# A priority offset of 200 for what side streams emit, in a two-block fp32 transformer kernel on one core

## The chip, the cores and the metric

One core of a Trainium2 chip. The metric is the device time of one execution in microseconds (us). TensorE is PE in the rows (its weight loads PEld), VectorE is DVE, ScalarE is ACT, GpSimd is POOL, SyncE is SP; every DMA of the kernel is issued from SP's queue.

## What is computed

A sequence of 256 tokens of width 1024, all in float32, goes through two blocks. Cut to what matters:

```
first_block:  cols = rmsnorm(x) @ w_in
              ya = rwkv7_time_mix(cols)       # 8 heads of 64, state S_t = S_{t-1} diag(w_t) + (S_{t-1} a_t) b_t^T + v_t k_t^T
              yb = diff_attention(cols)       # 4 heads, softmax(a) - lam * softmax(b), ALiBi
              x += (gates * (ya @ w_proj_a, yb @ w_proj_b)) @ w_out
              x += relu(rmsnorm(x) @ w_ff1)**2 @ w_ff2      # 1024 -> 4096 -> 1024
              x  = rmsnorm(x + gated per-layer embedding)
second_block: for layer in 0, 1:
                x += 0.5 * swiglu(rms_norm(x))              # 1024 -> 2816 -> 1024
                x += attention(rms_norm(x))   # layer 0: stick-breaking, MoBA; layer 1: forgetting, dilated; q and k normed and rotated
                x += 0.5 * swiglu(rms_norm(x))
```

## The kernel before

The 256 tokens are two tiles of 128. Each product with a weight matrix is three matmuls (`mm3`, which calls `mm`, L279): weight and activation are each split into a high and a low part, and hi by hi, hi by lo and lo by hi are summed in PSUM. Weights come in units of 128 x 1024 floats (512 KB). `wunit` (L336) issues the DMA into one of three `raw` buffers (L341), and `split` makes `hi` on ACT (L365) and `lo` on DVE (L366). There are five pairs of hi and lo buffers during the first mix, eleven after it. In the trace the same two lines also split the transposed activations (hTh, hTl).

The main stream is these products. What lies between them, the elementwise work of the two mixes and of the attentions with its small matmuls and transposes (`tr`, L283), is written as generators, the side streams. `Weave` (L126 to L205) keeps them: `spawn` (L163) starts one, `pump` takes the stream that is due first and lets `step` (L143) run it to its next `yield`, and `mm` calls for that as planned time passes. So the program order is a braid of main and side streams, which the planner's own clock makes.

PE runs in exactly the program's order, since a manual schedule is set for it. DVE, ACT, POOL and SP don't: the framework's scheduler orders their instructions, and among those that it deems ready it takes the one of highest priority, which is the one that stands first in the program. Once built, each engine's order is fixed, and an engine waits for the next instruction in its order, whatever else is ready behind it. Some streams are started before anything else, and some of what they emit is loads: `Mix.setup` (L1061, constants `fv`, `w2a`, `k_mix`, `g`), `setup_late` (L1096, `row_sub`), `bf_const` (`cb_alibi`, L308). The first activations are loaded in `first_part` (L1550, L1552), normed into `h` (L909) and transposed.

Names used below: `kk`, `c`, `AR`, `BK` and `X` belong to the time mix (`prepare`, L1174, and the inverse, L1267 on), `UV` to its chain over chunks (L1355), `oa` to its output (L1384, L1404), `gate` to the gates ahead of w_out (L1542, L1659), `qk` and `Q` to the first mix too (L1413, L1284). In the second block `qk_norm` (L542) norms q and k of one token tile (L548 to L565; its rotation `rb` is on POOL, L562 and L563), and `softmax_side` (L649) makes the weights that PE then transposes (maxima `m` L678, masked weights L685). Token tile 0 of that step in layer 1 has the tile w__11067, tile 1 has w__11112, and the first softmax tiles are w__11203 and w__11204; in layer 0 tile 1 is w__6776. `forget_sums` (L567) makes `fx` and `lf`.

Of the kernel before, what the change touches and what calls it, by code (L numbers as in the profile page):

```python
# [108 lines left out]
class Mark:  # L109


    def __init__(self):
        self.done, self.at, self.res = False, 0.0, None
# [8 lines left out]
class Weave:  # L122
# [20 lines left out]
    def step(self, s):  # L143
        t = self.t
        try:
            v = next(s.gen)
        except StopIteration as e:
            self.credit -= self.t - t
            self.finish(s, e.value or 0.0)
            if s in self.sides:  # L150
                self.sides.remove(s)
            return
        self.credit -= self.t - t
        s.wait, s.due = (), self.t
        if isinstance(v, float):
            s.due += v
        else:
            s.wait = tuple(v)
# [60 lines left out]
class Ker:  # L219


    def __init__(self, ctx, tc, d):
        self.tc, self.nc, self.d = tc, tc.nc, d
        nc = self.nc
        ctx.enter_context(tc.manual_schedule(engines={mybir.EngineType.PE}))
        self.W = Weave()
        self.const = ctx.enter_context(tc.tile_pool(name="const", bufs=1))
        self.xp = ctx.enter_context(tc.tile_pool(name="xp", bufs=1))
        self.act = ctx.enter_context(tc.tile_pool(name="act", bufs=2))
        self.ps = ctx.enter_context(tc.tile_pool(name="ps", bufs=1, space=PSUM))  # L230
        self.banks = Slots(self.W, self.ps, "b", [128, 512], 8)
        self.quota, self.held = 2, 0
        self.x = [self.xp.tile([128, D], F32, name=f"x{t}") for t in range(2)]
        self.pre = None
# [548 lines left out]
    def attn_layer(self, pool, hT, layer, after):  # L783
# [64 lines left out]
        for step, g in ATTN_ORDER:  # L848
            if step == "qk":
                queries(g, GROUPS.index(g))  # L850
            else:
                vms.setdefault(g, Mark())
                values(g)
# [100 lines left out]
def attn_plan(layer):  # L954
    win = "w_in_ab_2" if layer == 0 else "w_in_cd_2"
    out = []
    for step, g in ATTN_ORDER:
        a, b = g * 256, g * 256 + 256
        if step == "qk":
            out.append(((win, 0, ("qk", g)), (0, D), [(a, b), (D + a, D + b)]))  # L960
        else:
            more = [(3 * D, 3 * D + 8)] if layer == 1 and g == GROUPS[0] else []
            out.append(((win, 0, ("v", g)), (0, D), [(2 * D + a, 2 * D + b)] + more))
    for g in GROUPS:
        out.append((("w_out_2", layer, g), (g * 256, g * 256 + 256), [(0, D)]))
    return out
# [53 lines left out]
def mix_plan():  # L1020
    def attend(i):
        a, b = 1792 + i * 128, 1792 + i * 128 + 128
        return (("w_in", 0, ("at", i)), (0, D), [(a, b), (512 + a, 512 + b), (1024 + a, 1024 + b)])

    out = [attend(0), (("w_in", 0, "wg"), (0, D), [(1536, 1792)])]
    for j in range(4):
        a, b = j * 128, j * 128 + 128
        out.append((("w_in", 0, ("kr", j)), (0, D), [(512 + a, 512 + b), (a, b)]))
    for j in range(2):
        out.append((("w_in", 0, ("v", j)), (0, D), [(1024 + j * 256, 1280 + j * 256)]))  # L1030
    for step, i in MIX_ORDER:
        out.append(attend(i) if step == "at" else (("w_in", 0, ("gt", i)), (0, D), [(3328 + i * 512, 3840 + i * 512)]))
    out.append((("w_proj_b", 0, 0), (0, 512), [(0, D)]))
    out.append((("w_proj_a", 0, 0), (0, 512), [(0, D)]))
    out.append((("w_out", 0, 0), (0, D), [(0, D)]))
    return out
# [817 lines left out]
```

## Time and profile before

| | us |
|---|---|
| median of 3 runs | 1529.46 (1527.96 to 1530.95) |
| the profiled execution | 1529.78 |
| its span | 1528.0 |
| PE busy | 1489.4 (97%) |
| DVE busy | 927.9 (61%) |
| ACT busy | 760.8 (50%) |
| POOL busy | 46.7 (3%) |
| mean granted clock of PE | 0.994 |

The span runs from the first to the last instruction of the profile; the profiled execution's own time has 1.78 us around it. A row of the timeline gives start, duration, engine, line, operation, output and inputs with their sizes, and, in brackets, the idle time of the engine just before and what ended it.

### The profile page before, as it was taken

To read this page: it belongs to the slowest core of one execution; us is meant where nothing else is said; L and a number is where in the kernel's file an instruction comes from. 1 tells how busy PE (TensorE), PEld (TensorE's weight loads), DVE (VectorE), ACT (ScalarE), POOL (GpSimd) and SP (SyncE) were. 2 spreads that over 40 slices of the span, in tenths; PEclk is the share of its full clock that TensorE was granted. 3 is DMA by queue.
4 is the path that set the end of the run, shared out by engine and by line. 5 is a ranking of instruction groups with operands and counts; after the bars stand their busy time and mean duration, and the time that the engine had idled before them with its cause. 6 is when DMAs were issued, how large, how long until landed. Compare 5 with 4: busy or idle time off the path is not lost.

```text
span 1528.0 us, 22440 instructions
## 1 busy us (share of the span) xinstructions
PE 1489.4 (97%) x8804; PEld 1237.2 (81%) x8804; DVE 927.9 (61%) x1528; ACT 760.8 (50%) x1142; POOL 46.7 (3%) x70
## 2 busy tenths in 40 slices
PE   7999989999999999999999999999999999999999
PEld 6887767788888788887888888887888888888887
DVE  5886777755558755557546554566545787565552
ACT  6644445644536544447565444445444566464441
POOL 1120100000000000001100000000000010000000
PEclk9999999999999999999999999999999999999999
DMA  7233238655544765536434665547555444275551
GB/s 253 90 118 107 98 119 278 202 194 177 182 151 157 223 200 190 185 132 193 138 111 147 198 194 192 179 156 220 190 189 182 141 154 136 78 227 180 179 182 53
DMA packets 76298, 254.97 MB, mean 167 GB/s; under 512 B 11040, under 2 KB 13344, under 8 KB 76192
## 3 DMA queue, kind: packets, MB, share of 16 engines
q1 hardware_dynamic: 76192, 253.53, 51.1%
q8 instruction: 69, 1.13, 0.3%
q14 instruction: 37, 0.30, 0.1%
HBM read 252.45 MB, written 1.05 MB: 166 GB/s over the span
## 4 chain that ended last, share of the span: by engine, by line
PE 81%; DVE 7%; DMA 5%; ACT 4%; issue 2%; POOL 0%; SPq 0%; ACTq 0%; DVEq 0%; POOLq 0%
PE b L279 77%; DMA raw<-in_w_dram 4%; PE b L283 4%; DVE lo L366 2%; ACT hi L365 2%; DMA grow<-in_norm_mix_g_dram 0%; DMA stage<-in_consts_dram 0%; DMA lam<-in_lam_k_dram 0%; POOL rb L563 0%; POOL rb L562 0%; DVE hTl L366 0%; DVE c L1132 0%; DVE U L1260 0%; DVE u L1129 0%; ACT e L376 0%
## 5 line engine op out<-in xcount | busy, mean ns | idle before, releaser
L366 DVE TENSOR_TENSOR lo<-raw,hi 128x1024 fp32r<-128x1024 f32 (+1 forms) x465 | 561.9, 1214 | 356.1 <-ACT hi L365 350.1
L365 ACT ACTIVATE hi<-raw 128x1024 fp32r<-128x1024 f32 (+1 forms) x465 | 485.6, 1050 | 417.4 <-PE b L279 207.6
L279 PE MATMUL b<-hi,hTh 128*128 128x512 f32 (+2 forms) x1312 | 499.9, 381 | 0.7 <-ACT hi L365 0.7
L279 PE MATMUL b<-hi,hTl 128*128 128x512 f32 (+2 forms) x1312 | 489.9, 373 | 0.5 <-DVE hTl L366 0.5
L279 PE MATMUL b<-lo,hTh 128*128 128x512 f32 (+2 forms) x1312 | 489.7, 373 | 0.8 <-DVE lo L366 0.8
L279 PEld LDWEIGHTS b<-hi,hTl 128*128 128x128 f32 x1312 | 247.4, 189 | 47.8 <-DVE hTl L366 0.9
L279 PEld LDWEIGHTS b<-hi,hTh 128*128 128x128 f32 x1312 | 247.6, 189 | 46.1 <-issue 2.5
L279 PEld LDWEIGHTS b<-lo,hTh 128*128 128x128 f32 x1312 | 247.8, 189 | 44.2 <-DVE lo L366 1.5
L279 PE MATMUL b<-hi,aTh 128*128 128x512 f32 x480 | 191.6, 399 | 0.0
L279 PE MATMUL b<-hi,aTl 128*128 128x512 f32 x480 | 188.1, 392 | 0.0
L279 PE MATMUL b<-lo,aTh 128*128 128x512 f32 x480 | 187.4, 390 | 0.0
L279 PEld LDWEIGHTS b<-hi,aTl 128*128 128x128 f32 x480 | 90.1, 188 | 20.1
L279 PEld LDWEIGHTS b<-lo,aTh 128*128 128x128 f32 x480 | 90.3, 188 | 18.0
L279 PEld LDWEIGHTS b<-hi,aTh 128*128 128x128 f32 x480 | 90.2, 188 | 17.6
L463 ACT ACTIVATE a<-b,rsi_x 128x512 f32<-128x512 f32 (+1 forms) x52 | 34.4, 662 | 55.3 <-PE b L279 55.2
L365 ACT ACTIVATE aTh<-b 128x512 fp32r<-128x512 f32 (+1 forms) x64 | 36.3, 567 | 43.2 <-PE b L283 41.8
L465 DVE SCALAR_TENSOR_TENSOR a<-b,rsi_x,a 128x512 f32<-128x512 f32 (+1 forms) x52 | 37.2, 716 | 32.1 <-PE b L279 17.3
L366 DVE TENSOR_TENSOR aTl<-b,aTh 128x512 fp32r<-128x512 f32 (+1 forms) x64 | 41.8, 653 | 20.0 <-ACT aTh L365 19.7
L279 PE MATMUL b<-hi,hT1h 128*128 128x512 f32 (+1 forms) x128 | 53.4, 418 | 0.0
L279 PE MATMUL b<-lo,hT1h 128*128 128x512 f32 (+1 forms) x128 | 47.8, 373 | 0.6 <-DVE lo L366 0.6
L279 PE MATMUL b<-hi,hT1l 128*128 128x512 f32 (+1 forms) x128 | 47.4, 371 | 0.0
L365 ACT ACTIVATE hTh<-b 128x512 fp32r<-128x512 f32 (+1 forms) x48 | 25.2, 541 | 38.1 <-PE b L283 33.5
(582 smaller groups left out, 1293.6 us busy)
## 6 DMA issues: line engine op xcount, KB each, us to landing
raw<-in_w_dram SPq DMA_DIRECT2D x446, 512.0 KB, 4.2
raw<-in_w_dram SPq DMA_DIRECT2D x16, 384.0 KB, 3.4
grow<-in_norm_ffn_dram SPq DMA_DIRECT2D x4, 512.0 KB, 5.3
x<-in_x_dram SPq DMA_DIRECT2D x4, 256.0 KB, 6.2
x<-in_x_dram SPq DMA_DIRECT2D x2, 512.0 KB, 4.4
grow<-in_norm_mix_dram SPq DMA_DIRECT2D x2, 512.0 KB, 4.8
out_dram<-x SPq DMA_DIRECT2D x4, 256.0 KB, 2.0
raw<-in_w_dram SPq DMA_DIRECT2D x2, 396.0 KB, 3.6
```

The source lines that it names most:

```text
L279: self.nc.tensor.matmul(out=out, lhsT=lhsT, rhs=rhs, start=start, stop=stop, skip_group_check=skip)
L283: self.nc.tensor.transpose(out=out, in_=src, identity=self.ident)
L365: self.nc.scalar.activation(out=hi, in_=src, func=AF.Copy)
L366: self.nc.vector.tensor_tensor(out=lo, in0=src, in1=hi.bitcast(F32), op=ALU.subtract)
L463: nc.scalar.activation(out=a[t], in_=p, func=AF.Silu if kind == "swiglu" else AF.Relu, scale=hT[t].r)
L465: nc.vector.scalar_tensor_tensor(out=a[t], in0=p, scalar=hT[t].r, in1=a[t], op0=ALU.mult, op1=ALU.mult)
```

## The change

`Weave.step` wraps the advance of a generator in `self.first()`, which opens the framework's priority context with an offset of 200: what the stream emits until its next `yield` is ranked as if it stood 200 instructions earlier in the program. This concerns DVE, ACT, POOL and SP; PE's order is the same, instruction by instruction.

```diff
     def step(self, s):
         t = self.t
         try:
-            v = next(s.gen)
+            with self.first():
+                v = next(s.gen)
         except StopIteration as e:
...
         self.W = Weave()
+        self.W.first = lambda: tc.high_priority(offset=200)
```

The lines behind these are numbered one higher from L146 on, and two higher from L227 on, in the changed kernel. Three places of the order, of the kernel before and of the changed one.

SP, at the start of the program. Before:

```order
1 L1550 DMA x_69<-in_x_dram 128x512
2 L1552 DMA grow<-in_norm_mix_g_dram 128x512
3 L239 DMA ident<-in_consts_dram 128x128
4 L308 DMA cb_identb<-in_masks_dram 128x256
5 L1550 DMA x_69<-in_x_dram 128x512
6 L1552 DMA grow<-in_norm_mix_g_dram 128x512
7 L341 DMA raw<-in_w_dram 128x768 x3
8 L1550 DMA x_70<-in_x_dram 128x512 x2
9 L341 DMA raw<-in_w_dram 128x768
10 L1065 DMA fv<-in_fv_dram 128x34
```

Now:

```order
1 L310 DMA cb_alibi<-in_masks_dram 128x768
2 L324 DMA row_sub<-in_diff_subln_g_dram 128x128
3 L1067 DMA fv<-in_fv_dram 128x34
4 L1078 DMA w2a_337<-in_rwkv_w_dram 64x512
5 L1079 DMA w2a_337<-in_rwkv_a_dram 64x512
6 L1082 DMA k_mix<-in_consts_dram 128x674
7 L1090 DMA g_344<-in_rwkv_g_dram 128x512
8 L1552 DMA x_69<-in_x_dram 128x512
9 L1554 DMA grow<-in_norm_mix_g_dram 128x512
```

Seven loads of side streams stand ahead of the first load of x, which was the first DMA of the program.

DVE, around the first step of the time mix's inverse (X, L1276 before, L1278 now). Before:

```order
106 L1132 SCALAR_TENSOR_TENSOR c<-u,fv,c 128x255
107 L1204 SCALAR_TENSOR_TENSOR kk<-sq,kk 128x256
108 L1276 TENSOR_TENSOR X<-b,X 128x256
109 L1206 SCALAR_TENSOR_TENSOR kk<-c,fv,kk 128x256
110 L1193 TENSOR_SCALAR sq<-b 128x256
111 L1208 SCALAR_TENSOR_TENSOR AR<-kk,P 128x4x64
112 L1214 TENSOR_TENSOR BK<-kk,ai 128x2x128
113 L1217 TENSOR_TENSOR c<-c,a 128x256
```

Now:

```order
94 L368 TENSOR_TENSOR lo<-raw,hi 128x1024
...
97 L368 TENSOR_TENSOR lo<-raw,hi 128x768
...
104 L1206 SCALAR_TENSOR_TENSOR kk<-sq,kk 128x256
105 L1211 TENSOR_TENSOR AR<-c,P 128x4x64
106 L1208 SCALAR_TENSOR_TENSOR kk<-c,fv,kk 128x256
107 L1195 TENSOR_SCALAR sq<-b 128x256
108 L1210 SCALAR_TENSOR_TENSOR AR<-kk,P 128x4x64
109 L1216 TENSOR_TENSOR BK<-kk,ai 128x2x128
110 L1219 TENSOR_TENSOR c<-c,a 128x256
111 L1278 TENSOR_TENSOR X<-b,X 128x256
```

X goes from ahead of the other heads' chain (kk to c) to behind it, and the split of a 768-wide weight unit, which stood behind all this, is ahead of it.

DVE, in the attention of layer 1, where q and k of token tile 1 are normed. Before:

```order
1012 L405 SCALAR_TENSOR_TENSOR rsa_q<-qss,rsi_q 128x8
...
1019 L553 TENSOR_TENSOR qn<-b,rsi_q 128x512
1020 L614 COPY w__11361<-c_ones 128x4
1021 L366 TENSOR_TENSOR lo<-raw,hi 128x1024
1022 L564 TENSOR_TENSOR w__11112<-qn,gc 128x512
1023 L678 TENSOR_REDUCE m<-b 128x2
1024 L565 TENSOR_TENSOR w__11112<-w__11112,rb 128x512
1025 L685 SCALAR_TENSOR_TENSOR w__11203,l<-w__11203,cb_dcnt 128x128 x2
1026 L678 TENSOR_REDUCE m<-b 128x2
```

Now:

```order
1000 L687 SCALAR_TENSOR_TENSOR w__11203,l<-w__11203,cb_dcnt 128x128
1001 L687 SCALAR_TENSOR_TENSOR w__11204,l<-w__11204,cb_dcnt 128x128 x2
1002 L368 TENSOR_TENSOR lo<-raw,hi 128x1024
1003 L708 RECIPROCAL rl<-l 128x4
1004 L581 SCALAR_TENSOR_TENSOR lf<-fx,fe 128x8
1005 L407 SCALAR_TENSOR_TENSOR rsa_q<-qss,rsi_q 128x8
1006 L408 TENSOR_TENSOR rsa_q<-rsa_q,rsi_q 128x8
1007 L409 SCALAR_TENSOR_TENSOR rsi_q<-rsa_q,rsi_q 128x8
1008 L555 TENSOR_TENSOR qn<-b,rsi_q 128x512
1009 L566 TENSOR_TENSOR w__11112<-qn,gc 128x512
1010 L567 TENSOR_TENSOR w__11112<-w__11112,rb 128x512
```

The chain that ends in w__11112 stood ahead of the softmax steps; now the softmax steps of w__11203 and w__11204, three more weight splits and `lf` are ahead of it, from its second step (L405 before) on.

## Rows read from the trace of the kernel before

**Rows 1.** The page: busy time of PE, and the chain that ended last.

```profile
PE 1489.4 (97%) x8804; PEld 1237.2 (81%) x8804; DVE 927.9 (61%) x1528; ACT 760.8 (50%) x1142; POOL 46.7 (3%) x70
PE 81%; DVE 7%; DMA 5%; ACT 4%; issue 2%; POOL 0%; SPq 0%; ACTq 0%; DVEq 0%; POOLq 0%
```

**Rows 2.** Table by stretch: bounds, length, busy time (instructions) per engine, PE clock, DMA share, GB/s.

```profile
38.20:76.40 38.20, 34.42 (x306) 32.31 (x304) 31.75 (x68) 23.83 (x46) 5.61 (x12) 0.91 0.28 90
```

**Rows 3.** The waits of PE: total us, times, longest one.

```profile
PE b L279 <- DVE UV L1355: 3.5, 1, 3.5
...
PE b L279 <- DVE lo L366: 2.3, 3, 0.9
PE b L279 <- ACT kk L1182: 2.1, 2, 1.2
PE b L283 <- DVE gate L1659: 1.8, 2, 1.0
...
PE b L283 <- DVE w__6776 L565: 1.1, 1, 1.1
PE b L283 <- DVE oa L1404: 1.1, 1, 1.1
...
PE b L279 <- ACT Q L1284: 1.0, 1, 1.0
...
PE b L283 <- ACT qk L1413: 0.9, 2, 0.5
```

**Rows 4.** Table by stretch, around two idle times of PE, and at the start.

```profile
7.50:10.00 2.50, 0.00 (x0) 0.00 (x0) 0.77 (x2) 1.21 (x3) 0.00 (x0) 1.00 0.99 384
...
57.30:64.10 6.80, 6.80 (x34) 6.58 (x33) 6.17 (x15) 3.96 (x8) 0.19 (x1) 0.50 0.06 25
...
197.20:204.00 6.80, 5.19 (x21) 4.25 (x22) 6.31 (x23) 0.00 (x0) 0.00 (x0) 0.50 0.45 154
```

**Rows 5.** Timeline of SP: the first two issues of the program.

```profile
0.74 0.39 SPq L1550 DMA_DIRECT2D x<-in_x_dram  x1
1.18 0.42 SPq L1552 DMA_DIRECT2D grow<-in_norm_mix_g_dram  x1
```

**Rows 6.** DMA issues from 0 to 26 us: KB each, median us to landing.

```profile
k_mix<-in_consts_dram SPq DMA_DIRECT2D x1, 337.0 KB, 6.1
...
cb_alibi<-in_masks_dram SPq DMA_DIRECT2D x1, 192.0 KB, 3.7
```

**Rows 7.** Table by stretch: while the first half of x lands.

```profile
2.50:5.00 2.50, 0.00 (x0) 0.00 (x0) 0.29 (x1) 0.72 (x2) 2.07 (x6) 1.00 0.84 270
```

**Rows 8.** Timeline of DVE and PE around X.

```profile
66.43 1.29 DVE L1229 TENSOR_TENSOR G<-b,k_mix 128x512 f32<-128x512 f32 x2 [1.55 <-PE b L279]
...
75.84 0.42 DVE L1276 TENSOR_TENSOR X<-b,X 128x256 f32<-128x256 f32 x1
...
77.57 0.42 DVE L1217 TENSOR_TENSOR c<-c,a 128x256 f32<-128x256 f32 x1
...
76.43 0.75 PE L279 MATMUL b<-X,U 32*32 32x32 f32 x64
```

**Rows 9.** The page's costliest groups: the weight split on DVE, mean ns.

```profile
L366 DVE TENSOR_TENSOR lo<-raw,hi 128x1024 fp32r<-128x1024 f32 (+1 forms) x465 | 561.9, 1214 | 356.1 <-ACT hi L365 350.1
```

**Rows 10.** Timeline of DVE at w__6776, attention of layer 0.

```profile
713.46 0.69 DVE L565 TENSOR_TENSOR w__6776<-w__6776,rb 128x512 f32<-128x512 f32 x1 [0.28 <-POOL rb L563]
```

**Rows 11.** Timeline of DVE, POOL and PE around w__11112, attention of layer 1.

```profile
1225.83 0.69 DVE L565 TENSOR_TENSOR w__11112<-w__11112,rb 128x512 f32<-128x512 f32 x1 [0.30 <-POOL rb L563]
1226.44 0.29 DVE L685 SCALAR_TENSOR_TENSOR w__11203<-w__11203,cb_dcnt 128x128 f32<-128x128 f32 x1
...
1230.02 0.16 DVE L579 SCALAR_TENSOR_TENSOR lf<-fx,fe 128x8 f32<-128x8 f32 x1
...
1222.99 1.66 POOL L562 TENSOR_TENSOR rb<-qn,gs 128x256 f32<-128x256 f32 x1 [4.88 <-DVE w__11361 L614]
...
1226.76 0.60 PE L283 MATMUL b<-ident,w__11112 128*128 128x128 f32 x4
```

## The prediction

> **What bounds the kernel now.** I read the page first: PE is busy for 97% of the span, and 81% of the chain that ended last is PE's own work, with DVE (7%) and ACT (4%) behind [rows 1]. So DVE, ACT and SP cost time only where PE waits for what they make, and as PE's order does not change, the whole question is at which places of that fixed order PE finds its input earlier or later. The table by stretch says where such places are: in the first mix PE has 34.42 of 38.20 us, at a granted clock of 0.91 [rows 2]; the long MLP stretches have next to no idle time, and there the order of DVE only exchanges single splits that lie many microseconds ahead of their use. The list of PE's waits then names what is late: results of side streams (UV 3.5 us, kk 2.1, gate 1.8, w__6776 1.1, oa 1.1, Q 1.0, qk 0.9) and weight splits (lo, 2.3 in three waits) [rows 3]. That is under 14 us in all, so a priority for side streams has little to win. Last come the clock's rows: two stretches of 6.80 us that follow idle time of PE at about 54 and 195 us show a granted clock of 0.50, 1.2 GHz [rows 4].
>
> The sum is made against the profiled execution, 1529.78 us, 0.32 above the median of the runs shown. A change under 0.2%, 3.1 us, can't be told from none here.
>
> **Part 1, the start.** Before, the first DMA of the program is half of x, issued at 0.74 us, and the next follows 0.44 later [rows 5]. Now seven loads go first. Seven issues at 0.44 make 3.1 us. Their bytes, by the shapes in the order and the rows, are 337 KB (k_mix), 192 (cb_alibi) [rows 6], 256 (g), twice 128 (w2a) and some 80 in the two small ones: 1.12 MB. At the 270 GB/s that the engines moved while x landed that is 4.1 us, at the 384 of the next stretch but one 2.9 [rows 4, 7]. Issue and transfer overlap, so they are not added. PE has nothing to do before x is there, so nothing hides it: 2.9 to 5.2 us (both one behind the other in part), and I take **+3.7**. Nothing gives it back: the moved loads land earlier than before, but PE waited for none of them. The DVE work that goes ahead of the first `h` (row_sub, omm, oka) is small and its loads are issued ahead of x.
>
> The row for the first stretch shows engines already 84% busy at 270 GB/s [rows 7], so a load ahead of x takes x's place. The Trainium skill, DMA: Bandwidth & Descriptors, section "Rules for kernel authors", says the opposite for a load by itself: issue it early, compute, wait late. By that rule this term would be zero and the sum 3.7 us less. The same page, section "Where 436 GB/s comes from", puts the engines' ceiling at 435 GB/s, by which an estimate of the transfer is 2.6 us.
>
> **Part 2, the time mix, 45 to 90 us.** X feeds PE's next step with almost no slack: it ends at 76.26, and PE takes it at 76.43 [rows 8]. Now it stands behind the chain up to `c`, which ended 1.7 us later, at 77.99, and that chain itself comes later by the splits moved ahead of it (one of 1.2 us [rows 9], one of 768 columns, some 0.95). That is 3.9 in all, or 3.7 past the slack; where DVE idled before, 1.55 us at 66.43 [rows 8], part of the splits fits in. From 2.2 (all of it fits) to 3.7: I take **+3.2**. The earlier kk shortens PE's first wait in this stretch, by about half of the 2.1, but a few microseconds on PE waits for DVE again, so I count nothing for it.
>
> **Part 3, the rest of the mix to 265 us.** Here the streams do come earlier. Q goes ahead of a split on ACT, qk too: their 1.0 and 0.9 go. The gate products (L1659) pass two to three splits, so their 1.8 goes. UV's wait of 3.5 shrinks only by the half microsecond that moves behind it, since the work ahead of it is side work too. Against this, oa (L1404) falls behind four more activation splits, about 0.35 us each with no slack: +1.4. Together 1.4 − 1.0 − 0.9 − 1.8 − 0.5 = **−2.8** [rows 3]; from −4.2 (oa stays) to −0.5 (the gates' splits are missed instead).
>
> **Part 4, weight splits.** Two of lo's three waits, up to 0.9 each, fall away because the split is now earlier than side work: **−1.7** of the 2.3 [rows 3].
>
> **Part 5, attention of layer 0.** PE waits 1.1 us for w__6776, which ends at 714.15 [rows 3, 10]. Now one split (1.21) and a share of the next stand between its last two steps: 1.2 to 2.6, taken **+2.1**. Other shifts of this stage, of a microsecond and both signs, are left to the range.
>
> **Part 6, attention of layer 1.** This is the largest term. PE transposes w__11112 at 1226.76, 0.24 us after it is ready (1225.83 + 0.69), and in PE's order this comes ahead of the softmax tiles [rows 11]. Now its chain stands behind four masked weights (L685, 0.29 each), a maximum (0.4), three splits (1.2 each) and three ops of about 0.2: 5.8 us of work. By the other way of counting, the chain starts again only behind `lf`, at 1230.18, and then runs with nothing to overlap: three small steps (0.5), qn (0.7), the rotation on POOL, from 1222.99 to 1225.83 before (2.8), and the last step (0.7), which ends at 1234.9, 8.4 us later [rows 11]. `lf` itself can come somewhat sooner, so I take **+6.5**; the bounds are 4.5 and 8.2. The softmax tiles behind it are then long ready.
>
> **Part 7, the clock.** A wait of PE at 54 us and the 3.5 of UV at 195 were each followed by 6.8 us at half clock [rows 3, 4], 3.4 us of full-speed work lost where PE is busy throughout. Against this, at the start PE is idle for a whole stretch of 2.5 us and the row shows 1.00 [rows 4]. A wait of 6 us at 1226 is the longest of all; I take half of the 3.4, **+1.7** (0 to 6.8, if the wait at 714 brings one too).
>
> **The sum**: 3.7 + 3.2 − 2.8 − 1.7 + 2.1 + 6.5 + 1.7 = +12.7, so 1542.5 for an execution like the profiled one, 1542.2 beside the median. The good ends of all terms give 2.9 + 2.2 − 4.2 − 2.3 + 1.2 + 4.5 + 0 = +4.3 (1533.8), the bad ends 5.2 + 3.7 − 0.5 − 0.9 + 2.6 + 8.2 + 6.8 = +25.1 (1554.6).
>
> **The rivals.**
> (a) *The streams win*, faster. Every wait of [rows 3] goes, 13.8 us, and with UV's the half clock at 197 (3.4, [rows 4]). With the start's +3.7 that is −13.5: **1516.0**. It decides at UV and at w__11112: if DVE serves them before PE asks. For it: most of the waits are side streams' results. Against it: at X and w__11112 the order puts the awaited step later. Chance 0.15. (The Trainium skill, Perfetto Trace Analysis, section "Optimization Strategies", would have one speed up the engines that hold up the matmul engine, which is this way round; by the order that holds here for part 3 and not for parts 2, 5 and 6.)
> (b) *Only the start counts*: inside the run DVE is busy 61% of the time, gaps swallow the shifts, reliefs and losses cancel. 1529.8 + 3.7 = 1533.5, **1533.2** beside the median. Against it: DVE is full at the two places (no idle time in the rows from 75.84 to 77.57). Chance 0.13.
> (c) *Nothing shows*: the seven loads move in time that x's own landing leaves, and the rest cancels. **1529.5**. Against it: engines 84% busy [rows 7]. Chance 0.09. (It is what the skill's rule on early loads in part 1 would bring.)
> (d) *Late splits and a slow clock on top*: each new wait brings its 6.8 us at 1.2 GHz, and PE's waits for weights grow. The bad ends: **1554**. Chance 0.07.
>
> **How the numbers follow.** The forecast, 1542, has 0.56, and its own range is 1533.8 to 1552. Faster is (a) and a little of (c): 0.16. Within 0.2%: (c), and where (b) has a smaller start: 0.10. Slower: the rest, 0.74. Leaving out (a) and (d) leaves out about 2 in 10, so the range is 1529 to 1552.
>
> **What would show it.** In the trace after: x issued near 4 us instead of 0.74; a wait of PE for X (L1278) of some 3 us near 80 us; waits for gate, Q and the lo splits gone; UV's still near 3 us with its half clock; a wait for w__11112 (L567) of 5 to 8 us near 1235, the longest after the start, perhaps with a new stretch at 0.50. Wrong would be: x landing as early as before (part 1), or no wait at w__11112 because its steps met DVE idle (part 6); without part 6 and its clock the time is near 1534.

## The result, and the profile after

The changed kernel took 1556.33 us (median of 4 executions, 1554.2 to 1558.6) beside 1530.07 for the kernel before on the same chip (4 executions): a ratio of 1.0173, with a 95% interval of 1.0156 to 1.0189. It is slower, as forecast, but by 26 us where 12.7 had been worked out. The profiled execution took 1555.25 us, its span 1553.3, 25.3 above the span before.

The page of the changed kernel has these two lines, busy time by engine and the chain that ended last:

```profile
PE 1494.5 (96%) x8804; PEld 1239.6 (80%) x8804; DVE 932.5 (60%) x1528; ACT 763.6 (49%) x1142; POOL 47.4 (3%) x70
...
PE 75%; DVE 9%; DMA 7%; ACT 5%; issue 3%; POOL 1%; SPq 0%; ACTq 0%; DVEq 0%; POOLq 0%
```

No engine has more work than before [rows 1]: the counts are equal. PE is busy for 5.1 us more. Its stretches at 0.50 come to 27.2 us (six of 3.4, one of 6.8) against 17.0 before, and it is busy for 23.2 and 15.4 us of them, so half of the 7.8 more, 3.9 us, is the clock. The other 20.2 of the 25.3 us are idle time of PE, 58.8 us against 38.6. With them grew the part of the chain that lies outside PE, from 19% to 25%. The list of PE's waits (us in total, times, longest) names them:

```profile
PE b L285 <- DVE h L911: 12.7, 3, 11.5
PE b L285 <- DVE w__11112 L567: 7.3, 1, 7.3
PE b L285 <- DVE w__6776 L567: 3.6, 1, 3.6
PE b L281 <- DVE X L1278: 2.9, 1, 2.9
PE b L285 <- DVE oa L1406: 2.7, 1, 2.7
...
PE b L285 <- DVE a L467: 2.3, 3, 0.8
PE b L281 <- ACT kk L1184: 2.1, 2, 1.8
PE b L281 <- DVE UV L1357: 2.0, 2, 1.4
...
PE b L285 <- ACT w__12147 L378: 1.5, 1, 1.5
PE b L285 <- DVE w__11361 L560: 1.4, 1, 1.4
PE b L281 <- ACT tw L1145: 1.4, 1, 1.4
PE b L281 <- DVE lo L368: 1.3, 2, 0.7
```

Against [rows 3], UV went from 3.5 to 2.0, lo from 2.3 to 1.3, and gate, Q and qk are gone from the top of the list. But X, w__11112, w__12147, w__11361 and tw are new there, and w__6776 and oa have grown. The 11.5 for h is the start, where the kernel before has one wait of 3.6 and one of 5.5.

Since PE runs the same 8804 matmuls in the same order in both kernels, each matmul can be looked up in both traces, and the difference of its starts is the delay up to there. This table has it at the matmuls where the delay changes (us; the last column is the growth since the row above):

```text
before    after     delay   growth  what PE met on the way
14.31     17.83     +3.5    +3.5    the start: x lands later
35.03     37.63     +2.6    -0.9
80.09     88.42     +8.3    +5.7    tw +1.4, kk +2.0, X +2.9 and its clock +1.5, the rest -2.1
90.00     97.15     +7.2    -1.2    a lo split that is no longer late
262.13    270.51    +8.4    +1.2    UV and its clock -4.4, oa and its clock +3.2, gate -2.2, hTh and hTl +2.0, their clock +1.6, UV +.8, lo +.8, Q -.8
519.19    525.01    +5.8    -2.6    an activation at 513 -2.5 and its clock -1.6, small losses +1.5
700.17    706.04    +5.9    +0.1
718.02    727.38    +9.4    +3.5    w__6776, with a stretch at half clock
772.09    783.44    +11.4   +2.0    w__7418, a softmax tile
1030.09   1042.49   +12.4   +1.1    an activation at 870
1042.01   1052.45   +10.4   -2.0    a lo split that is no longer late
1225.13   1236.58   +11.4   +1.0    an activation at 1062
1233.19   1251.92   +18.7   +7.3    w__11112, with a stretch at half clock
1307.08   1328.02   +20.9   +2.2    w__11361, softmax tiles
1314.09   1339.42   +25.3   +4.4    w__12147, w__12148, with a stretch at half clock
```

From there to the end the delay stays at 25.3.

At the start, SP issues seven loads ahead of x; the first, the last and x:

```profile
0.74 0.39 SPq L310 DMA_DIRECT2D cb_alibi<-in_masks_dram  x1
...
3.98 0.43 SPq L1090 DMA_DIRECT2D g<-in_rwkv_g_dram  x1
4.45 0.43 SPq L1552 DMA_DIRECT2D x<-in_x_dram  x1
```

x goes out 3.71 us later than before [rows 5], and the first products of h come 3.5 us later.

DVE around X, in its timeline:

```profile
76.90 1.45 DVE L368 TENSOR_TENSOR lo<-raw,hi 128x768 fp32r<-128x768 f32 x1
...
82.45 0.41 DVE L1219 TENSOR_TENSOR c<-c,a 128x256 f32<-128x256 f32 x1
82.79 0.41 DVE L1278 TENSOR_TENSOR X<-b,X 128x256 f32<-128x256 f32 x1
```

X now follows `c` at once, as the order said, and lies 6.95 us later than before [rows 8]; PE waits 2.9 us for it.

DVE, then PE and POOL, around w__11112:

```profile
1240.37 1.22 DVE L368 TENSOR_TENSOR lo<-raw,hi 128x1024 fp32r<-128x1024 f32 x1 [0.23 <-ACT hi L367]
...
1241.60 0.14 DVE L581 SCALAR_TENSOR_TENSOR lf<-fx,fe 128x8 f32<-128x8 f32 x1
...
1244.95 0.69 DVE L567 TENSOR_TENSOR w__11112<-w__11112,rb 128x512 f32<-128x512 f32 x1 [1.28 <-POOL rb L565]
...
1243.09 1.16 POOL L564 TENSOR_TENSOR rb<-qn,gs 128x256 f32<-128x256 f32 x1 [13.32 <-DVE qn L555]
...
1245.70 1.12 PE L285 MATMUL b<-ident,w__11112 128*128 128x128 f32 x4 [7.33 <-DVE w__11112 L567]
```

The chain starts again only behind `lf`, and from there to its end takes 1241.60 to 1245.64, 4.0 us, with DVE idle for 1.28 of them while POOL rotates.

Two of the stretches at half clock, in the table by stretch (columns as in [rows 2]):

```profile
1241.70:1248.50 6.80, 2.80 (x10) 2.40 (x11) 2.52 (x7) 0.60 (x1) 1.83 (x2) 0.50 0.38 116
...
1333.80:1337.20 3.40, 3.40 (x14) 3.01 (x13) 0.85 (x2) 0.40 (x2) 0.00 (x0) 0.50 0.00 1
```

The last place of the table is one that no row shown so far covers. ACT before, at the softmax tile w__12147 (timeline):

```profile
1307.09 0.47 ACT L376 ACTIVATE w__12147<-b,m 128x256 f32<-128x256 f32 x1 [1.89 <-DVE m L678]
...
1307.56 0.47 ACT L376 ACTIVATE w__12147<-b,m 128x256 f32<-128x256 f32 x1
```

and now:

```profile
1328.03 0.47 ACT L378 ACTIVATE w__12147<-b,m 128x256 f32<-128x256 f32 x1 [1.89 <-DVE m L680]
...
1328.49 0.41 ACT L367 ACTIVATE hTh<-oT 128x256 fp32r<-128x256 f32 x1
1328.80 1.05 ACT L367 ACTIVATE hi<-raw 128x1024 fp32r<-128x1024 f32 x1
1329.75 0.37 ACT L831 ACTIVATE oT<-b 128x256 f32<-128x256 f32 x1
1330.01 0.72 ACT L367 ACTIVATE hTh<-oT 128x256 fp32r<-128x256 f32 x2
1330.63 0.47 ACT L378 ACTIVATE w__12147<-b,m 128x256 f32<-128x256 f32 x1
```

Between the two exponentials of one tile, which stood back to back, there are now a weight split (`hi`), three activation splits (`hTh`, here the main stream's too, L865 before) and a copy: 2.60 us from start to start instead of 0.47. PE's transpose then waits 1.47 us for that tile and 0.69 for the next. It is a side stream's work that is made late, by main-stream work. A priority for side streams should do the opposite.

### The profile page after: what moved, and what is told of

Read it like the earlier page. It is cut to its first block, busy times and chain, and to the rows that moved or that the text cites. A ratio compares the mean times of both kernels' runs of the same rounds, so it can differ in the third digit from the quotient of the medians.

```text
span 1553.3 us, 22488 instructions
## 1 busy us (share of the span) xinstructions
PE 1494.5 (96%) x8804; PEld 1239.6 (80%) x8804; DVE 932.5 (60%) x1528; ACT 763.6 (49%) x1142; POOL 47.4 (3%) x70
## 4 chain that ended last, share of the span: by engine, by line
PE 75%; DVE 9%; DMA 7%; ACT 5%; issue 3%; POOL 1%; SPq 0%; ACTq 0%; DVEq 0%; POOLq 0%
PE b L281 71%; DMA raw<-in_w_dram 6%; DVE lo L368 4%; PE b L285 4%; ACT hi L367 3%; DVE hTl L368 0%; DMA x<-in_x_dram 0%; POOL rb L564 0%; POOL rb L565 0%; ACT L374 0%; DVE m L680 0%; DVE a L467 0%; ACT hTh L367 0%; DVE c L1134 0%; ACT e L378 0%
## 5 line engine op out<-in xcount | busy, mean ns | idle before, releaser
L465 ACT ACTIVATE a<-b,rsi_x 128x512 f32<-128x512 f32 (+1 forms) x52 | 34.4, 661 | 49.7 <-PE b L281 49.6
L368 DVE TENSOR_TENSOR hTl<-b,hTh 128x512 fp32r<-128x512 f32 (+1 forms) x48 | 28.7, 619 | 29.7 <-ACT hTh L367 29.5
```

Of the source, the lines that this page charges most:

```text
L368: self.nc.vector.tensor_tensor(out=lo, in0=src, in1=hi.bitcast(F32), op=ALU.subtract)
L465: nc.scalar.activation(out=a[t], in_=p, func=AF.Silu if kind == "swiglu" else AF.Relu, scale=hT[t].r)
```

## The experiments

What that points to can be read from the program. The order shown ahead of the prediction already holds it: of the seven loads ahead of x, six are `setup`'s and `setup_late`'s (L1061, L1096), which the main stream calls (L1579, L1589) and no side stream emits, though the text there counts them among what streams emit. The framework keeps a counter that ranks each instruction as it is emitted. Opening the priority context lowers it by 200, and leaving the context sets it back. But a stream's last step leaves the `with` block by the exception that ends a generator, and then the counter is not set back. Read while the program is built, it goes from 56 to −138 at the end of the first stream, then to −332, −517 and −711 at the next three; the build has 169 such ends, and the counter finishes near −24,700. So the description of the change ahead of the prediction, that only what a stream emits until its next `yield` is ranked higher, is what the code reads like and not what it does: with each stream's end all that is emitted later, the main stream's splits and loads included, ranks some 200 higher against what was emitted earlier and still waits, side streams' chains among it, and this adds up from end to end.

The letters in the expectations stand for theories: L is that the offset left behind at the ends is the cost, W that within it the weight splits which pass the chains carry most; others are rivals, told in the quotes.

**The context closed at a stream's end too.** The exception is caught inside the block:

```diff
-        try:
-            with self.first():
+        end = None
+        with self.first():
+            try:
                 v = next(s.gen)
-        except StopIteration as e:
+            except StopIteration as e:
+                end = e
+        if end is not None:
```

> The priority context is closed also when a stream ends, so the offset holds for what a side stream emits and for nothing else. Theory L (the offset is left behind at each stream's end, so all later text, the main stream's weight splits and loads included, ranks 200 higher again and again): the first load of x is first again, w__11112 and w__6776 are made before the softmax steps, and the time is 1527 to 1534 us, no change. Theory S (ranking the streams' own results up is what costs): most of the 26 us stays, 1545 to 1556.

Measured: 1528.01 against 1529.55, a ratio of 0.9988 (0.9975 to 1.0000). Its list of PE's waits:

```profile
PE b L288 <- DVE gate L1664: 3.1, 2, 1.9
...
PE b L284 <- DVE X L1281: 2.5, 1, 2.5
PE b L284 <- DVE UV L1360: 2.3, 2, 1.8
```

w__11112, w__6776, w__12147 and oa are gone from its top, and x is issued at 0.74 us again. The priority for side streams, done as the change describes it, is worth nothing that can be told apart here. All of the 26 us hang on the counter. One wait stays without making the kernel slower: by the streams' own rank X stands behind `c` here too, and PE waits 2.5 us for it.

**Only the offset left behind.** No priority for streams at all; the kernel before, with one line at the exception:

```diff
         except StopIteration as e:
+            self.tc.cur_priority -= 200
```

> No priority for what streams emit, but 200 taken off the priority counter whenever a stream ends. Theory L: as the changed kernel, 1550 to 1560 us, with the seven loads ahead of x and a wait of 6 to 8 us at w__11112. Theory S: as before, 1527 to 1535.

Measured: 1560.57, a ratio of 1.0211 (1.0188 to 1.0235). The offset left behind alone makes the whole loss, and a little more. The two long waits are there on sister tiles:

```profile
PE b L285 <- DVE w__11067 L567: 4.8, 1, 4.8
PE b L285 <- DVE w__6731 L567: 4.5, 1, 4.5
```

**Left behind in one block only.** The changed kernel, with 200 added back at each stream's end from `second_block` on:

```diff
         except StopIteration as e:
+            if self.restore:
+                self.tc.cur_priority += 200
...
+    K.W.restore = True
     second_block(K, out, hF)
```

> The changed kernel in the first block; in the second block the counter is set right at each stream's end. Theory L: the delay against the kernel before that the changed kernel shows where the first attention begins, 5.9 us, stays to the end: 1536 us, 1533 to 1539. Theory S: the second block keeps its losses, 1550 to 1558.

Measured: 1543.91, 1.0093 (1.0074 to 1.0113), some 5 us above what was expected. At the same matmuls its delay is 8.7 at 262 us and 10.9 at 508, near the changed kernel's 8.4 and 9.9, but 11.6 at 519, where the changed kernel has 5.8. The relief of 4.1 that the changed kernel has there (2.5 the wait for an activation `a`, 1.6 its half clock) did not come. DVE in this run, and then in the changed kernel:

```profile
518.60 0.23 DVE L542 TENSOR_TENSOR gc<-grow,stage 128x64 f32<-128x64 f32 x1 [0.64 <-DMA stage<-in_consts_dram]
...
524.23 0.75 DVE L470 SCALAR_TENSOR_TENSOR a<-b,rsi_g,a 128x512 f32<-128x512 f32 x1 [0.95 <-ACT a L468]
```

```profile
519.90 0.75 DVE L467 SCALAR_TENSOR_TENSOR a<-b,rsi_g,a 128x512 f32<-128x512 f32 x1
...
525.13 0.22 DVE L539 TENSOR_TENSOR gc<-grow,stage 128x64 f32<-128x64 f32 x1
```

`gc` is a constant that `second_block` makes for its first attention (L537 before). Here, as in the kernel before, it stands ahead of the last norm of the first block, on which `a` depends, and waits for a load; in the changed kernel it stands behind. So the relief belongs to what the second block's ends do, which this run sets right, and the expectation was wrong to count it with the first block. From 519 us to the end nothing is added: 11.6 and 11.7. The other half, restored in the first block and left behind in the second:

> The counterpart of the third run: set right at each stream's end in the first block, left behind in the second. If the two blocks' losses simply add, the changed kernel's 26 us less the third run's 14.4 is left: 1541 to 1545 us, with waits at w__6776, w__7418, w__11112, w__11597 and w__12147 as in the changed kernel. If the first block's delay shifts what collides in the second: under 1538 or over 1548.

Measured: 1545.36, 1.0108 (1.0089 to 1.0127), just above what was expected. It has the second block's two longest waits of the changed kernel:

```profile
PE b L288 <- DVE w__11112 L570: 7.4, 1, 7.4
...
PE b L288 <- DVE w__6776 L570: 3.2, 1, 3.2
```

Both tiles belong to `second_block`. The halves give 14.4 and 16.3, 30.7 together, for 26.3 of both, each uncertain by about 3 us. In the traces, cut at 508 us, they add: with the first block left behind 10.9 us are lost up to there and 0.8 after it, with the second 1.7 are gained and 15.8 lost, and in the changed kernel 9.9 and 15.4 are lost.

**The start by itself.** The kernel before, with `setup`'s five loads (0.87 MB by the shapes) ranked ahead of x:

```diff
-        self.setup()
+        with K.tc.high_priority(offset=3000):
+            self.setup()
```

> The kernel before, with five of the seven loads (setup's, 0.87 MB) ahead of the first load of x and nothing else moved on purpose. If the loads are the start's price: 5 issues of 0.44 us or 0.87 MB at 270 GB/s, 2.2 to 3.2 us, so 1532 to 1533.5 us. If another thing made the changed kernel's start late: 1529 to 1531.

Measured: 1532.8, 1.0023 (1.0011 to 1.0036): 3.2 us for five loads, with x issued at 3.51 us:

```profile
3.51 0.43 SPq L1550 DMA_DIRECT2D x<-in_x_dram  x1
```

That is 2.77 later than before [rows 5]. In its trace the delay at PE's matmuls is 3.2 at 20 us, falls to 1.2 from 250 to 500, and is 3.5 at the end, after a longer wait for the activation at 513 and a half-clock stretch at 1232 that the kernel before does not have. So the loads' price is shown where it is paid; that it lasts to the end by itself is not.

**The splits put back.** The changed kernel, offset left behind as it is, but each weight split (its `hi` on ACT and `lo` on DVE) ranked 1000 lower:

```diff
+        p = self.tc.cur_priority
+        self.tc.cur_priority = p + 1000
         self.split(hi[:, :n], lo[:, :n], raw[:, :n])
+        self.tc.cur_priority = p + 2
```

> The changed kernel, but each weight split (hi on ACT, lo on DVE) is ranked 1000 places later than its place in the program; the offset is still left behind at each stream's end. Theory W (the leftover offset costs because weight splits pass the side chains): in the attentions the waits at w__6776, w__7418, w__11597 and w__12147 go back to those of before and w__11112's falls from 7.5 to about 2 us; the start's 3.5 us and oa's stay: 1534 to 1541 us. Theory R (it is later side streams that pass earlier ones, whatever the splits do): the waits stay and the time is 1550 to 1557.

Measured: 1534.38 against 1530.52, 1.0025 (1.0011 to 1.0039). Of the 26 us 22 are gone, which bears W out. What is left in its list of waits:

```profile
PE b L285 <- DVE oa L1409: 2.7, 1, 2.7
...
PE b L285 <- DVE w__6776 L570: 1.9, 1, 1.9
...
PE b L281 <- DVE X L1281: 1.2, 1, 1.2
```

In its trace the start costs 2.9 us and oa 3.2, while w__11112, w__7418 and w__11597 cost nothing in the end: the first two come from loads and activation splits that moved, not from weight splits. Not all that was expected to go went: 0.8 of w__6776's loss, 1.5 at w__11361 and 1.7 of the 4.4 at w__12147 and w__12148 are still there.

**The splits put back, without the change.** Would the same rule, 100 lower, help the kernel before?

> The kernel before, with no priority for streams at all; each weight split ranked 100 places later. If the waits of before were side results behind splits: UV, BK and gate come 2 to 4 us earlier, their waits and one or two stretches at 1.2 GHz go, 1518 to 1525 us. If the order among the streams was the cause: 1527 to 1532. If lo at 85 us comes later instead, its wait grows by about 1.4 us.

Measured: 1529.91, 0.9998 (0.9987 to 1.0009): no. UV's wait gives 3.8 us back and BK's 4.0, each with its half clock, but

```profile
PE b L279 <- DVE lo L369: 5.9, 6, 2.9
...
PE b L279 <- ACT Q L1287: 2.2, 1, 2.2
```

the splits that were put back are now late themselves, and Q's wait has grown from 1.0.

**Ranks that serve UV.** UV's wait of 3.5 us, with its half clock, was the largest inside the span [rows 3, 4]. Four kernels tried to win it. First the closed context, with 600 for the streams `inverse` and `chain` and 200 for the others:

```diff
+        self.W.first = lambda n: tc.high_priority(offset=600 if 'inverse' in n or 'chain' in n else 200)
```

> The context closed at each stream's end, as in the first run, and the offset 600 for the time mix's inverse and chain, 200 for the other streams. Theory L: with nothing left behind, the streams that PE waits for can be put ahead of the rest: the wait for UV (3.5 us before) and its stretch at 1.2 GHz go, X is no longer behind the other heads' chain (2.5 us in the first run), the wait for gate near 250 us (about 2 us more in the first run) stays: 1519 to 1525 us. Theory S (ranking up doesn't help): 1527 to 1533.

Measured: 1534.88, 1.0029 (1.0016 to 1.0041), missed. UV's wait is gone, and lo, the split that now stands behind UV's chain, takes its place (4.8 us):

```profile
PE b L284 <- DVE lo L371: 5.5, 2, 4.8
```

The same with `flip_side` at 30 and the splits 100 lower:

```diff
+        self.W.first = lambda n: tc.high_priority(offset=600 if 'inverse' in n or 'chain' in n else 30 if 'flip_side' in n else 200)
...
+        self.tc.cur_priority = p + 100
         self.split(hi[:, :n], lo[:, :n], raw[:, :n])
```

> As the run before this one, with the offset 30 for streams that transpose (flip_side), and each weight split ranked 100 places later. The waits for gate go too (1.8 us before, more in the closed version), and lo's in the mix don't come back, since the splits that were late before are not behind side work now: 1512 to 1520 us. If the splits then come late for PE: new waits for lo or hi in the first 90 us and 1522 or more.

Measured: 1532.6, 1.0012 (0.9998 to 1.0027), missed. PE does not wait for UV any more, and its timeline behind DVE's shows the exchange:

```profile
202.55 2.36 DVE L374 TENSOR_TENSOR lo<-raw,hi 128x1024 fp32r<-128x1024 f32 x2
...
203.83 0.79 PE L284 MATMUL b<-lo,hT1h 128*128 128x512 f32 x1 [4.82 <-DVE lo L374]
```

Then exact ranks without the context: `chain` 600 up, `diff_out` 400 down, all else as before.

```diff
+        up = 600 if 'chain' in n else -400 if 'diff_out' in n else 0
+        self.tc.cur_priority -= up
```

> The kernel before with exact ranks (the counter goes back by as much as it was lowered): the chain 600 up, the norm and the transposes of the differential attention's output (diff_out) 400 down, all else untouched. If DVE is full from 185 to 204 us, so that a stream put ahead only pays if another that PE doesn't wait for goes behind the splits: UV's wait (3.5 us) and its stretch at 1.2 GHz go and no wait for lo takes their place, oa loses about 1.5 us: 1523 to 1527 us. If any order of that stretch costs the same: a new wait of 3 us or more between 190 and 225 us, 1528 to 1533.

Measured: 1532.66, 1.0018 (1.0005 to 1.0030), missed. UV's wait and its stretch are gone (6.1 us), but dP, oa and the gates come later (2.85, 3.35 and 3.0 by the matmuls that take them, each with a half-clock stretch of 3.4 behind it):

```profile
182.52 0.74 PE L289 MATMUL b<-ident,dP 128*128 128x128 f32 x3 [1.72 <-DVE dP L1458]
...
221.56 0.66 PE L289 MATMUL b<-ident,oa 128*128 128x128 f32 x2 [3.05 <-DVE oa L1410]
```

And with a rank for every stream of the mix (`inverse` and `chain` 600, flips 30, what is given out 0 or −400, others 200):

> As the run before this one, and the inverse 600 up, the other streams of the time mix and the attentions 200 up, transposing streams 30 up, with exact ranks. BK comes 2.6 us earlier on DVE (its wait of 1.7 and the stretch at 1.2 GHz go), X 1.4 us earlier, kk on ACT about 1 us later: 2 to 5 us less than the run before, 1519 to 1525. If DVE and ACT are full from 45 to 90 us as well: what BK and X win comes back as waits for kk and lo, no less than the run before.

Measured: 1531.34, 1.0006 (0.9993 to 1.0019). Its delay is −5.8 at 205 us, −2.2 at 230 and −1.8 at 1225, but then a short wait is followed by a long stretch at half clock, and 5.6 us are lost at once (PE's timeline, and the table by stretch). The profiled execution, 1534.96, is among the slowest of its twelve:

```profile
1227.51 0.59 PE L289 MATMUL b<-ident,w__11204 128*128 128x128 f32 x2 [1.07 <-DVE w__11204 L691]
...
1228.60:1238.80 10.20, 9.50 (x35) 7.36 (x36) 5.25 (x21) 3.76 (x9) 0.00 (x0) 0.50 0.39 135
```

**Closed, with the flips low.** Of the 169 streams 106 are `flip_side`, which only transpose and split activations. The closed context, with an offset of 10 for these and 200 for the others:

```diff
+        self.W.first = lambda n: tc.high_priority(offset=10 if 'flip_side' in n else 200)
```

> The closed version of the first run, with the offset 10 instead of 200 for streams that only transpose and split (flip_side). The gate's waits of that run (3.4 us around 250) shrink by 1.5 to 2.5 and the rest of its order stays: 1525 to 1528 us, faster than before by 0.1 to 0.3%. If the work that goes ahead instead only moves the wait on, as it did with UV: 1527 to 1531.

Measured: 1526.32 against 1529.01 (12 and 17 executions), 0.9982 (0.9968 to 0.9996). Its waits for X and UV are those of the closed version, 2.5 and 2.3, and the gates' is 1.2 less, a little under what was expected:

```profile
PE b L288 <- DVE gate L1664: 1.9, 1, 1.9
```

It is the one of the twelve kernels tried whose interval lies below 1, with a median 0.18% lower. That is about the smallest difference this measurement tells from none, and the interval of the plainly closed version overlaps its own, so whether the flips' rank matters stays open.

## Why the prediction was right and wrong

The sign was right, and so was the way of looking: PE's order is fixed, and the loss lies where PE finds its input later. The sign came from the rows of the new order, which already held the counter's fault; from the change as it is described there, the closed version, no loss would have followed (0.9988). Part by part:

- **The start (part 1)** was put at +3.7; the first matmuls came 3.5 later, and the five loads of the experiment alone cost 3.2. Nothing hid them at the start, and the rival in which nothing shows falls with that. "Nothing gives it back" is not shown: in the trace with five loads 2 of the 3.2 us were made up by 250 us and lost again at other places. The Trainium skill, DMA: Bandwidth & Descriptors, section "Rules for kernel authors", has one issue loads early and wait late; the runs do not bear that out for loads that stand ahead of the one that PE waits for, since these cost 3.2 us (five) and 3.5 us (seven).
- **X (part 2)**: the mechanism held, X stands behind `c` and PE waits 2.9 us. The stretch cost +5.7 instead of +3.2, because the splits in front also delayed tw and kk (+1.4 and +2.0), which I had counted at nothing, and because X's wait has 3.4 us at half clock behind it (+1.5); 2.1 came back at other places.
- **The rest of the mix (part 3)** was the first step that failed: −2.8 forecast, +1.2 measured. Gains were there (UV and its clock 4.4, Q 0.8). oa cost 3.2 instead of 1.4: its wait grew by 1.65, near the forecast, and a half-clock stretch at 227.9 made the rest. The gates' own waits went, as forecast (−2.2), but the activation splits hTh and hTl behind them came 2.0 late with another half-clock stretch (+1.6), +1.4 in all instead of −1.8. Later waits for UV and lo cost +0.8 each.
- **The splits (part 4)**: −1.7 forecast, −1.2 and −2.0 at two places, 3.2 together.
- **w__6776 (part 5)**: +2.1 forecast, +3.5 measured with a half-clock stretch of 3.4 us, which the forecast had as a bad end only.
- **w__11112 and the clock (parts 6 and 7)**: +6.5 and +1.7 forecast, +7.3 measured with its stretch at half clock. This part was right.
- **"Other shifts of this stage, of a microsecond and both signs, are left to the range" (part 5)** is the step that failed most. Added up, the places that no part priced (w__7418, the two activations at 870 and 1062, w__11361, the softmax tiles up to 1307, w__12147 and w__12148) are 2.0 + 1.1 + 1.0 + 2.2 + 4.4 = 10.7 us. They are not of both signs. In each of them a weight split of the main stream has gone ahead of a step on ACT or DVE, so they come from one cause; the steps are softmax and norm steps of side streams, and the two activations, products of the MLPs that the main stream itself makes (`a`, L465 before). Of the MLP stretches the prediction had said that the order of DVE only exchanges single splits there; where a split passes `a`, at 870 and 1062, PE waits 0.8 us for it. Against them stands one relief at 513, −2.6 up to 519.

The differences from the forecast, of the table's rows: −1.1 before 35 us, +2.5 for X's stretch, −1.5 for the splits, +4.0 for the rest of the mix, −2.6 up to 519, +0.1, +1.4 at w__6776, −0.9 at w__11112 and +10.7 elsewhere, 12.6 in all, which is what the sum lacked.

The list of waits was short, too: "under 14 us in all" leaves out BK (1.7), qkT (1.8), qss (1.2) and the activations `a` (2.7), all of them in the list of PE's waits before.

Behind this is a rival that I did not list: that the change does not do what it says. I had the evidence, since the loads of `setup` ahead of x were the first thing in the order, and I took them for loads of side streams. Read rightly they say that the main stream had been raised too, and then every side stream's chain on a full DVE or ACT is in danger, with one sign. The rival that the streams win, 1516, fell for the same cause; with the context closed they do come first, and the time is 0.9988 of before: a gain of at most 0.25%. The Trainium skill, Perfetto Trace Analysis, section "Optimization Strategies", has one optimize the engines that hold up the matmul engine; the five kernels that did so by ranks for UV's chain or for the splits measured 0.9998 to 1.0029, each with another step late in the place of the one that was served. The rival of late splits and a slow clock at 1554 was nearest in time, but it had 0.07 and the wrong step: the weight splits were early, not late.

Not settled: what sets where a half-clock stretch falls and how long it lasts; whether the start's delay alone reaches the end; and whether the 0.18% of the last version would hold in more executions.

## What to carry to other kernels

A context that changes the order of what follows has to be closed on every way out, and a generator's end is an exception: look in the new order for work that the change should not have moved, and ask who emits it, before any of it is priced. Where the order shifts everywhere in one direction, price every step with less slack than the shift, ACT's included; here the small ones, of one cause, added and did not cancel. And where DVE is full, giving a late step a better place moves the wait to the step that it passed (UV's 3.5 us became 4.8 for lo), so four rankings that removed the largest wait won nothing.

## What was not expected of the hardware

A wait of PE is sometimes followed by a stretch at a granted clock of 0.50 (1.2 GHz), and how long it lasts does not follow the wait: 10.2 us after a wait of 1.07 in one experiment, 6.8 about one of 7.3 in the changed kernel, 3.4 after 1.5 and 0.7. The same order does not fix it either: the kernel with the offset left behind in the first block only has, in the mix, the changed kernel's order of DVE and ACT row by row, and 10.2 us at half clock at 57.5 where the changed kernel had 3.4 at 64.1. Single executions of one kernel scatter with the clock: those of the closed version lie between 1523.38, at a mean granted clock of 0.998, and 1530.42, at 0.995, and the profiled one was the lowest. One profile can thus show where a wait is, and still be several microseconds off in what it costs; a tenth of a per cent needs the median of many executions.
